# A hybrid attention and feed-forward block on one core: decays from empty rows, gate sums on quarters of the array, S1 in its own tile

## The chip, the cores and the metric

One Trainium2 chip, one core. The metric is the device time of one execution in microseconds, the median of several runs. The profile is of one execution, taken by the hardware profiler.

## The reference

One layer on x of 1024 frames by 1024 channels, all in float32. What matters here is the gated linear attention: 4 heads, 16 chunks of 64 frames each.

```
a = rmsnorm(x); proj = a @ w_in      # q, k, v, r, a_low (16), su, sv, g_gla, g_sgu
logit = a_low @ w_gate_up + b_gate
log_a = log_sigmoid(logit) / 16      # (16 chunks, 64 frames, 4 heads, 128)
cum = cumsum(log_a) in each chunk;  tot = cum[last frame]
k_dec = k * exp(tot - cum);  upd = k_dec^T v (each chunk);  decay = exp(tot)
state = decay * state + upd;  o = q @ state   (every frame reads its chunk's end state)
```

Behind it come a normalisation of o and silu(r), a spatial gating unit on su and sv, two branch projections that are gated and added, w_out, and a SwiGLU block (w_ffn_in, w_ffn_out); both halves add to x through a normalisation.

## The kernel before

Every large product is a pair of output blocks made with seven block products in place of eight (class `Pair`): the input is split in quadrants a11, a12, a21, a22, sums of quadrants such as S1 = a21 + a22 are formed, and products m1 to m7 are accumulated. Each operand of a product is a rounded part (fp32r, written by ScalarE, line 85) and the rest (written by VectorE, line 86), so that one product of 128 x 128 by 128 x 512 is three matmuls (lines 109 to 111: high by high, low by high, high by low; tiles ah and al for the mixer's input, hh and hl for the feed-forward's). The first two pairs run in the order 1, 2, 5, 7, 6, 4, 3, two pairs in turn. `Stream.run(n, fill)` issues n products and after each steps background generators: the decays, the rows of k, the scan and others put their matmuls between the products. The order on each engine is set by the framework's scheduler from the priorities that this order of issue gives and from when operands are expected; `tc.issue_after` holds something back behind a named instruction.

Of the input, `tile` (line 159) transposes four blocks of 128 columns into the raw quadrants, `first` splits a11 and a12 (operands of m1 and m2), `second` (line 177) splits a22 (operand 4), adds a21 to a22 in place (line 181) and splits the sum (operand 5), and `rest` (line 184) forms operands 7, 6 and 3 from the sum, by subtractions in place.

The low-rank gate input (16 columns of w_in): `low_rank_weights` loads them, forms differences and splits them into `wah`, 64 columns of weights; `low_rank_sums` (line 457) makes two halves with 16 matmuls each from the split operands 1, 2, 5 and 4. They are called behind the fourth and the sixth product. `low_rank` (line 460) loads `w_gate_up` and `b_gate` into `wg` with three transfers of GpSimd's queue, and copies the sums into `al`, 96 rows: high part, low part, ones. `decays` (line 479) goes head by head: eight matmuls of 96 rows give the logits (line 491, tile lg), ScalarE takes Abs, Exp and Ln, VectorE the minimum and difference (line 500), the result is split (lh, ll). Then 16 matmuls with `chunksr` of two columns sum each chunk (line 508, tile tot) and ScalarE exponentiates them into `decay`; 4 matmuls with the strictly lower matrix `laterr` give the sums over later frames (lines 517, 518, tile gg), whose exponentials go to HBM (kd_d, line 390) and come back in `k_rows` (tile kdl), where k is scaled.

`scan` (line 537) takes two blocks of 128 frames in a round p: `update` (line 559, tile u, two banks) on halves of the array's rows, four state steps on VectorE (line 577), four readouts (line 586, tile o, one bank) on halves of its columns, then transpositions (ot). Small products share a pool of four PSUM banks (`tbank`).

The feed-forward input goes the same way (tiles hraw, hh, hl, `Hs`), with `Hs.rest` behind six products.

Of the kernel before, what the change touches and what calls it, by code (L numbers as in the profile page):

```python
# [8 lines left out]
F32 = mybir.dt.float32  # L9
F32R = mybir.dt.float32r  # L10
# [21 lines left out]
def hybrid_block(ctx, tc, I, out):  # L32
# [20 lines left out]
    kd_d = dram("kd_d", [HEADS, P, S])  # L53
    u_d = dram("u_d", [KT, P, S])
# [87 lines left out]
    class Operands:  # L142
# [34 lines left out]
        def second(self, tt):  # L177
            cols = slice((tt % 4) * P, (tt % 4) * P + P)
            a21, a22 = (self.raw[1, c][:, :, cols] for c in range(2))
            self.put(4, a22, cols)  # L180
            nc.vector.tensor_tensor(out=a22, in0=a21, in1=a22, op=ALU.add)
            self.after = self.put(5, a22, cols)

        def rest(self):
            a11, a12, a21, s1 = self.raw[0, 0], self.raw[0, 1], self.raw[1, 0], self.raw[1, 1]
# [122 lines left out]
    class Stream:  # L308
# [58 lines left out]
    chunks = cst.tile([P, 2], F32, name="chunks")  # L367
    nc.vector.memset(chunks, 0.0)
    nc.vector.memset(chunks[0:64, 0:1], 1.0 / 16)
    nc.vector.memset(chunks[64:128, 1:2], 1.0 / 16)  # L370
    chunksr = cst.tile([P, 2], F32R, name="chunksr")
    nc.vector.tensor_copy(chunksr, chunks)
    decay = cst.tile([P, HEADS, NT * 2], F32, name="decay")
# [66 lines left out]
    def low_rank_weights():  # L440

        wa = pl.tile([P, 12, 16], F32, tag="L", name="wa")
        nc.gpsimd.dma_start(out=wa[:, 0:8], in_=w_in[:, OA : OA + 16].rearrange("(k p) c -> p k c", p=P))
        wah = pl.tile([P, 12, 64], F32R, tag="L", name="wah")
        nc.gpsimd.tensor_copy(wah, zero.broadcast_to([P, 12 * 64]).rearrange("p (k c) -> p k c", k=12))
        with tc.issue_after(A.after[1].ins):
            nc.vector.tensor_tensor(out=wa[:, 8:12], in0=wa[:, 4:8], in1=wa[:, 0:4], op=ALU.subtract)
            split(wah[:, :, 0:16], wah[:, :, 32:48], wa)
        low["w"] = wah

    def low_rank_sums(half, terms):

        low[half] = tbank(f"al_{half}")
        for n, (m, c) in enumerate(terms):
            for i in range(8):
                k, part = i // 2, A.hl[m][i % 2]
                nc.tensor.matmul(low[half][0:64], lhsT=low["w"][:, c * 4 + k, :], rhs=part[:, k],
                                 start=n == 0 and i == 0, stop=n == 1 and i == 7)

    def low_rank():  # L460
        with tc.issue_after(A.last.ins):
            al = slot("al", (96, S))
            nc.gpsimd.memset(al[64:96, :], 1.0)
            wg = slot("wg", (96, 512))
            nc.gpsimd.memset(wg, 0.0)
            nc.gpsimd.dma_start(out=wg[0:16, :], in_=I["w_gate_up"][0])
            nc.gpsimd.dma_start(out=wg[32:48, :], in_=I["w_gate_up"][0])
            nc.gpsimd.dma_start(out=wg[64:65, :], in_=I["b_gate"][0:1, :])
            vr = slot("vr", (24, P))
            nc.gpsimd.dma_start(out=vr[0:8], in_=I["sgu_ln_g"][0].rearrange("g (c p) -> (g c) p", p=P))  # L470
            nc.gpsimd.dma_start(out=vr[8:16], in_=I["sgu_ln_b"][0].rearrange("g (c p) -> (g c) p", p=P))
            nc.gpsimd.dma_start(out=vr[16:24], in_=I["gla_norm"][0].rearrange("g (c p) -> (g c) p", p=P))
        b = tbank("vecT")
        nc.tensor.transpose(b[:, 0:24], vr, ident[0:24, 0:24])
        nc.vector.tensor_copy(vecs, b[:, 0:24])
        for half in range(2):
            nc.scalar.activation(al[0:64, half * 512 : half * 512 + 512], low[half][0:64], AF.Copy)
        return al, wg

    def decays(al, wg):  # L480
        lh = slot("lh", (P, 1024), F32R)
        ll = slot("ll", (P, 1024), F32R)
        e = slot("e")
        for h in range(HEADS):
            lgs = []
            for q in range(2):
                lg = tbank(f"lg_{h}{q}")
                lgs.append(lg)
                for j in range(4):
                    tt = q * 4 + j  # L490
                    nc.tensor.matmul(lg[:, j * P : (j + 1) * P], lhsT=al[:, tt * P : (tt + 1) * P],
                                     rhs=wg[:, h * P : (h + 1) * P], start=True, stop=True)
                nc.scalar.activation(e[:, q * 512 : q * 512 + 512], lg, AF.Abs)
            yield
            yield
            nc.scalar.activation(e, e, AF.Exp, scale=-1.0)
            nc.scalar.activation(e, e, AF.Ln, bias=ones)
            for q in range(2):
                cols = slice(q * 512, q * 512 + 512)
                nc.vector.scalar_tensor_tensor(out=e[:, cols], in0=lgs[q], scalar=0.0, in1=e[:, cols], op0=ALU.min,  # L500
                                               op1=ALU.subtract)
# [602 lines left out]
```

## Time and profile before

| | |
|---|---|
| median of 3 runs | 1580.73 us (1579.82 to 1582.79) |
| profiled execution | 1581.19 us |
| its span, first to last instruction | 1579.3 us |
| mean granted TensorE clock | 0.991 of full |
| busy: TensorE, VectorE, ScalarE, GpSimd | 1545.6, 1134.2, 659.1, 168.2 us |
| instructions | 19738, of which 7103 matmuls |

The profile gives, for each engine, the time in which it worked; TensorE's matmuls overlap, so the duration of one (0.39 us for 512 columns) is longer than the distance to the next. The granted clock is the share of the full TensorE clock (2.4 GHz) that the chip allowed in a stretch; it has two levels here, full and half (1.2 GHz). An idle time in front of an instruction is shown with the instruction that ended it.

### The profile page before, as it was taken

The page shows a single profiled execution, that of the slowest core. Times are in us where ns is not written, and L with a number is a line of the kernel's source. Part 1 is how long each engine was busy: PE and PEld are TensorE (multiplying, and loading weights), DVE is VectorE, ACT ScalarE, POOL GpSimd, SP SyncE. Part 2 cuts the span into 40 slices and gives each one's busy share as a digit, 9 for nine tenths or more (in the row PEclk, how much of TensorE's full clock was granted, in tenths as well). Part 3 has the DMA queues.
Part 4 walks back from the last instruction along what each step waited for, and adds up shares of the span by engine and source line. Part 5 has one row for each costly group of instructions (what it writes and reads, how often), then busy time and mean ns, then how long its engine had stood idle before and what let it go on. Part 6 is the DMA issues. An engine that isn't in the chain of part 4 may idle for free.

```text
span 1579.3 us, 19738 instructions
## 1 busy us (share of the span) xinstructions
PE 1545.6 (98%) x7103; PEld 1261.5 (80%) x7103; DVE 1134.2 (72%) x1856; ACT 659.1 (42%) x1073; POOL 168.2 (11%) x251
## 2 busy tenths in 40 slices
PE   7999999999999999999999989999999999999997
PEld 5688777777788888888887877888888888888886
DVE  7855666767698788657697779787777776565547
ACT  8466433435444443444343654333333333354442
POOL 2100011112021112000000120111111100000001
PEclk9999999999999999999999998999999999999999
DMA  4232253636546455498982532565655543785653
GB/s 162 76 100 94 94 173 108 200 101 219 167 163 199 127 173 154 164 333 289 334 289 89 183 128 74 182 203 178 192 187 190 184 134 108 272 281 168 223 168 127
DMA packets 181236, 275.92 MB, mean 175 GB/s; under 512 B 10249, under 2 KB 108065, under 8 KB 181138
## 3 DMA queue, kind: packets, MB, share of 16 engines
q1 hardware_dynamic: 157714, 190.35, 38.1%
q0 software_dynamic: 23424, 84.30, 14.6%
q8 instruction: 56, 0.92, 0.2%
q14 instruction: 42, 0.34, 0.1%
HBM read 188.37 MB, written 86.25 MB: 174 GB/s over the span
## 4 chain that ended last, share of the span: by engine, by line
PE 91%; DVE 4%; ACT 2%; DMA 1%; issue 1%; POOL 0%; SPq 0%; DVEq 0%; POOLq 0%; ACTq 0%
PE f_m L110 9%; PE f_m L109 9%; PE f_m L111 9%; PE fo L109 4%; PE fo L111 4%; PE fo L110 4%; PE g_m L111 3%; PE g_m L109 3%; PE g_m L110 3%; PE kq_m L109 2%; PE v_m L110 2%; PE su_m L109 2%; PE v_m L109 2%; PE v_m L111 2%; PE sv_m L109 2%; PE kq_m L110 2%
## 5 line engine op out<-in xcount | busy, mean ns | idle before, releaser
L109 PE MATMUL f_m<-hh,w_f 128*128 128x512 f32 x616 | 241.2, 392 | 7.0 <-ACT hh L85 7.0
L110 PE MATMUL f_m<-hl,w_f 128*128 128x512 f32 x616 | 240.4, 391 | 0.0
L111 PE MATMUL f_m<-hh,w_f 128*128 128x512 f32 x616 | 238.2, 391 | 0.0
L109 PEld LDWEIGHTS f_m<-hh,w_f 128*128 128x128 f32 x616 | 116.3, 189 | 32.1 <-ACT hh L85 8.0
L110 PEld LDWEIGHTS f_m<-hl,w_f 128*128 128x128 f32 x616 | 116.4, 189 | 24.2
L111 PEld LDWEIGHTS f_m<-hh,w_f 128*128 128x128 f32 x616 | 116.2, 189 | 24.2
L111 PE MATMUL fo<-fow,foa 128*128 128x512 f32 x308 | 119.8, 389 | 0.0
L110 PE MATMUL fo<-fow,foa 128*128 128x512 f32 x308 | 119.8, 389 | 0.0
L109 PE MATMUL fo<-fow,foa 128*128 128x512 f32 x308 | 118.2, 389 | 0.0
L85 ACT ACTIVATE w_f<-wsum_f 128x512 fp32r<-128x512 f32 x88 | 55.4, 630 | 107.1 <-PE f_m L111 60.5
L109 PE MATMUL g_m<-ah,w_g 128*128 128x512 f32 x224 | 88.3, 394 | 0.0
L111 PE MATMUL g_m<-ah,w_g 128*128 128x512 f32 x224 | 87.8, 393 | 0.0
L110 PE MATMUL g_m<-al,w_g 128*128 128x512 f32 x224 | 87.7, 392 | 0.0
L85 ACT ACTIVATE w_f<-raw_f 128x512 fp32r<-128x512 f32 x66 | 41.4, 630 | 103.2 <-PE f_m L111 88.8
L86 DVE TENSOR_TENSOR foa<-fora,foa 128x1024 fp32r<-128x1024 f32 (+1 forms) x42 | 47.6, 1133 | 43.2 <-ACT foa L85 43.0
L85 ACT ACTIVATE foa<-fora 128x1024 fp32r<-128x1024 f32 (+1 forms) x42 | 41.5, 988 | 75.4 <-DMA fora<-fs_d 66.1
L274 DVE TENSOR_TENSOR f_o<-f_m,f_u 128x512 f32<-128x512 f32 x62 | 42.7, 689 | 40.2 <-PE f_m L111 40.0
L86 DVE TENSOR_TENSOR w_f<-wsum_f,w_f 128x512 fp32r<-128x512 f32 x88 | 60.4, 687 | 14.6 <-ACT w_f L85 14.1
L111 PEld LDWEIGHTS fo<-fow,foa 128*128 128x128 f32 x308 | 57.8, 188 | 12.1
L110 PEld LDWEIGHTS fo<-fow,foa 128*128 128x128 f32 x308 | 57.8, 188 | 12.1
L109 PEld LDWEIGHTS fo<-fow,foa 128*128 128x128 f32 x308 | 57.8, 188 | 11.8
L86 DVE TENSOR_TENSOR w_f<-raw_f,w_f 128x512 fp32r<-128x512 f32 x66 | 45.4, 688 | 21.0 <-ACT w_f L85 19.9
(384 smaller groups left out, 3743.0 us busy)
## 6 DMA issues: line engine op xcount, KB each, us to landing
raw_f<-in_w_ffn_in SPq DMA_DIRECT2D x88, 256.0 KB, 3.4
fora<-fs_d SPq DMA_DIRECT2D x35, 512.0 KB, 4.5
w2e<-in_w_ffn_out SPq DMA_DIRECT2D x44, 256.0 KB, 4.4
fs_d<-f_o POOLq DMA_DIRECT2D x22, 512.0 KB, 3.2
ws_d<-w2e POOLq DMA_DIRECT2D x22, 512.0 KB, 3.7
forw<-ws_d SPq DMA_DIRECT2D x20, 512.0 KB, 4.7
raw_g<-in_w_in SPq DMA_DIRECT2D x16, 512.0 KB, 4.6
g_d<-g_o POOLq DMA_DIRECT2D x16, 512.0 KB, 4.0
```

The source lines that it names most:

```text
L85: a = nc.scalar.activation(hi, src, AF.Copy)
L86: return a, nc.vector.tensor_tensor(out=lo, in0=src, in1=hi, op=ALU.subtract)
L109: nc.tensor.matmul(acc, lhsT=lh, rhs=rh, start=first, stop=False, skip_group_check=onto)
L110: nc.tensor.matmul(acc, lhsT=lh, rhs=rl, start=False, stop=False, skip_group_check=onto)
L111: nc.tensor.matmul(acc, lhsT=ll, rhs=rh, start=False, stop=last, skip_group_check=onto)
L274: tt(out=o, in0=in0, in1=in1, op=ALU.add)
```

## The change

1. S1 gets a tile of its own (quad(2, 0)); the split of a22 moves out of `second` into a new `fourth`, which is called behind the low-rank sums (and, for the feed-forward input, behind four products).
2. The low-rank sums are 32 plain f32 matmuls on raw quadrants with 32 columns of weights, each quarter of the array's columns taking 256 frames, issued behind the fourth product and before operand 4. The splits of the weights go. VectorE evacuates the bank once, adding 1 in the rows that carry the bias.
3. The logits are made for two heads at once, on quarters of the array's rows, in four banks; `wg` is loaded by eight transfers instead of three. A dependency by hand lets the first matmul of a pair of heads wait until all four banks are free.
4. The chunk totals (`tot`) go. The column of `later` that belongs to the last frame of each chunk, which was empty, is set to 1/16, so that row 63 (and 127) of gg holds the total, and its exponential the decay. Those rows are stored to `dec_d`, the other 63 rows of each chunk to kd_d, whose missing rows are filled with ones. Behind the fourth head `dt` is loaded from `dec_d` and one transposition (decT) brings the decays into place.
5. `update` of the next round is issued right behind the readouts of this one.

```diff
         def second(self, tt):
             cols = slice((tt % 4) * P, (tt % 4) * P + P)
-            a21, a22 = (self.raw[1, c][:, :, cols] for c in range(2))
-            self.put(4, a22, cols)
-            nc.vector.tensor_tensor(out=a22, in0=a21, in1=a22, op=ALU.add)
-            self.after = self.put(5, a22, cols)
+            s1 = self.quad(2, 0)[:, :, cols]
+            nc.vector.tensor_tensor(out=s1, in0=self.raw[1, 0][:, :, cols], in1=self.raw[1, 1][:, :, cols], op=ALU.add)
+            self.after = self.put(5, s1, cols)
+
+        def fourth(self, tt):
+            cols = slice((tt % 4) * P, (tt % 4) * P + P)
+            self.put(4, self.raw[1, 1][:, :, cols], cols)
...
+    for c in range(2):
+        nc.gpsimd.memset(later[c * 64 : c * 64 + 64, c * 64 + 63 : c * 64 + 64], 1.0 / 16)
...
+    def low_rank_sums():
+
+        low["al"] = tbank("al")
+        for k in range(KT):
+            for j in range(4):
+                a = A.raw[1 - j // 2, k // 4][:, k % 4, j % 2 * 256 : j % 2 * 256 + 256]
+                nc.tensor.matmul(low["al"][j * 32 : j * 32 + 32, 0:256], lhsT=low["w"][:, k], rhs=a, start=k == 0,
+                                 stop=k == KT - 1)
...
+            nc.vector.tensor_reduce(out=bias, in_=ident[:, 16:P:32], op=ALU.add, axis=mybir.AxisListType.X)
+            nc.vector.tensor_scalar(out=al, in0=low["al"][:, 0:256], scalar1=bias, scalar2=None, op0=ALU.add)
+        nc.gpsimd.memset(wg, 0.0)
+        for j in range(4):
+            nc.gpsimd.dma_start(out=wg[j * 32 : j * 32 + 16, :], in_=I["w_gate_up"][0])
+            nc.gpsimd.dma_start(out=wg[j * 32 + 16 : j * 32 + 17, :], in_=I["b_gate"][0:1, :])
...
+        for c in range(2):
+            nc.gpsimd.dma_start(out=kd_d[:, c * 64 + 63], in_=allone[0:HEADS])
...
+            for i in range(2):
+                for j in range(4):
+                    rows = slice(j * 32, j * 32 + 32)
+                    with tc.issue_after(first.ins) if first else ExitStack():
+                        mm = nc.tensor.matmul(lgs[j][:, i * 256 : i * 256 + 256], lhsT=al[rows, i * P : (i + 1) * P],
+                                              rhs=wg[rows, h * P : (h + 2) * P], start=True, stop=True)
...
-            tot = tbank(f"tot_{h}")
-            for tt in range(NT):
-                for part, first in ((lh, True), (ll, False)):
-                    nc.tensor.matmul(tot[:, 2 * tt : 2 * tt + 2], lhsT=part[:, tt * P : (tt + 1) * P], rhs=chunksr,
-                                     start=first, stop=not first)
-            nc.scalar.activation(decay[:, h], tot[:, 0 : NT * 2], AF.Exp)
...
-            store(kd_d[h], kd)
+            for c in range(2):
+                store(kd_d[h, c * 64 : c * 64 + 63], kd[c * 64 : c * 64 + 63])
+                store(dec_d[h, c : c + 1], kd[c * 64 + 63 : c * 64 + 64])
             yield
+            yield
+            yield
+        dt = slot("dt", (HEADS * 16, P))
+        nc.gpsimd.dma_start(out=dt, in_=dec_d.rearrange("h c (t k) -> (h c t) k", k=P))
+        for _ in range(4):
+            yield
+        b = tbank("decT")
+        nc.tensor.transpose(b[:, 0 : HEADS * 16], dt, ident[0 : HEADS * 16, 0 : HEADS * 16])
+        nc.vector.tensor_copy(decay.rearrange("p h c t -> p (h c t)"), b[:, 0 : HEADS * 16])
...
+        ubs = update(0)
+        yield
         for p in range(NT // 2):
             tt = 2 * p
-            ubs = update(tt)
-            yield
...
                 for i in (2, 1, 0):
                     read(i)
+                if tt + 2 < NT:
+                    ubs = update(tt + 2)
...
-    stream.run(4)
     low_rank_weights()
-    low_rank_sums(1, ((1, 0), (2, 1)))
+    stream.run(4)
+    low_rank_sums()
+    for tt in (0, 1, 2, 3):
+        A.fourth(tt)
     stream.run(2)
-    low_rank_sums(0, ((5, 0), (4, 2)))
     A.rest()
...
-    fstream.run(6)
+    fstream.run(4)
+    fstream.prepare(6)
+    for tt in (0, 1, 2, 3):
+        Hs.fourth(tt)
     Hs.rest()
```

The instructions on TensorE around the first change. Names: su0_m5 is the accumulator of product 5 of the first su pair, ah5 and al5 the two parts of operand 5, al_434 the bank of the low-rank sums. Before, behind the last product of m1 and m2:

```order
L110 MATMUL su1_m1_390<-al2_189,w_su12_270 128x512
L111 MATMUL su1_m1_390<-ah2_188,w_su12_270 128x512
L109 MATMUL su0_m5_472<-ah5_299,w_su05_407 128x512
L109 MATMUL su1_m5_492<-ah5_299,w_su15_426 128x512
L109 MATMUL su0_m7_554<-ah7_526,w_su07_469 128x512
L109 MATMUL su1_m7_571<-ah7_526,w_su17_489 128x512
L110 MATMUL su0_m5_472<-al5_300,w_su05_407 128x512
L111 MATMUL su0_m5_472<-ah5_299,w_su05_407 128x512
```

In the changed kernel the end of the low-rank sums stands at that place:

```order
L452 MATMUL al_434<-araw01_179,wa_363 32x256 x2
L452 MATMUL al_434<-araw11_289,wa_363 32x256 x2
L452 MATMUL al_434<-araw01_179,wa_363 32x256 x2
L110 MATMUL su0_m5_482<-ah5_293,w_su05_398 128x512
L110 MATMUL su1_m5_502<-ah5_293,w_su15_417 128x512
L110 MATMUL su0_m7_547<-ah7_519,w_su07_479 128x512
L110 MATMUL su1_m7_564<-ah7_519,w_su17_499 128x512
L111 MATMUL su0_m5_482<-al5_294,w_su05_398 128x512
```

The 32 low-rank matmuls stood 39 rows further on, all in one piece; they now stand between m2 and the first products of m5 and m7.

The second place on TensorE, before: the chunk totals of the first head among the kq products.

```order
L111 MATMUL kq0_m7_769<-ah4_294,w_kq04_809 128x512
L109 MATMUL kq0_m7_769<-ah4_294,w_kq04_809 128x512
L110 MATMUL kq0_m7_769<-al4_295,w_kq04_809 128x512
L508 MATMUL tot_0_845<-chunksr_125,ll_752 128x2
L508 MATMUL tot_0_845<-chunksr_125,lh_751 128x2
L508 MATMUL tot_0_845<-chunksr_125,ll_752 128x2
```

In the changed kernel there are none; the transposition of the decays stands among v products, ahead of the transpositions of k (kt):

```order
L112 MATMUL v1_m6_1308<-ah6_527,w_v16_1253 128x512
L110 MATMUL v1_m6_1308<-ah6_527,w_v16_1253 128x512
L111 MATMUL v1_m6_1308<-al6_528,w_v16_1253 128x512
L541 MATMUL decT_1291<-ident_106,dt_1250 128x64
L553 MATMUL kt_00_1297<-ident_106,kq0_o0_842 128x128 x4
L112 MATMUL v1_m6_1308<-ah6_527,w_v16_1253 128x512
L110 MATMUL v1_m6_1308<-ah6_527,w_v16_1253 128x512
```

Between the last gg matmul and decT the new order has 56 regular matmuls.

The third place, on TensorE in the scan of the first head, rounds 0 and 1, before. The last of four readouts and the next update:

```order
L586 MATMUL o_00_1474<-st_000_1450,kq0_o1_842 64x256
L111 MATMUL su2_m1_1516<-ah1_184,w_su21_1456 128x512
L109 MATMUL su2_m1_1516<-ah1_184,w_su21_1456 128x512
L110 MATMUL su2_m1_1516<-al1_185,w_su21_1456 128x512
L111 MATMUL su2_m1_1516<-ah1_184,w_su21_1456 128x512
L109 MATMUL su2_m1_1516<-ah1_184,w_su21_1456 128x512
L110 MATMUL su2_m1_1516<-al1_185,w_su21_1456 128x512
L111 MATMUL su2_m1_1516<-ah1_184,w_su21_1456 128x512
L559 MATMUL u_020_1531<-v_00_1382,kk_0_1349 128x256
L559 MATMUL u_021_1532<-v_00_1382,kk_0_1349 128x256
L559 MATMUL u_020_1531<-v_00_1382,kk_0_1349 128x256
L559 MATMUL u_021_1532<-v_00_1382,kk_0_1349 128x256
```

And in the changed kernel:

```order
L608 MATMUL o_00_1439<-st_003_1416,kq0_o1_860 64x256
L608 MATMUL o_00_1439<-st_002_1415,kq0_o1_860 64x256
L608 MATMUL o_00_1439<-st_001_1414,kq0_o1_860 64x256
L608 MATMUL o_00_1439<-st_000_1413,kq0_o1_860 64x256
L581 MATMUL u_020_1444<-v_00_1329,kk_0_1296 128x256
L581 MATMUL u_021_1445<-v_00_1329,kk_0_1296 128x256
L581 MATMUL u_020_1444<-v_00_1329,kk_0_1296 128x256
L581 MATMUL u_021_1445<-v_00_1329,kk_0_1296 128x256
```

The seven products between the readouts and the next update are gone; such neighbours were 5 before and are 12 now.

## Rows read from the trace of the kernel before

**Rows 1.** the page, busy time of each engine, and the chain's shares by engine
```profile
PE 1545.6 (98%) x7103; PEld 1261.5 (80%) x7103; DVE 1134.2 (72%) x1856; ACT 659.1 (42%) x1073; POOL 168.2 (11%) x251
...
PE 91%; DVE 4%; ACT 2%; DMA 1%; issue 1%; POOL 0%; SPq 0%; DVEq 0%; POOLq 0%; ACTq 0%
```

**Rows 2.** waits by engine: engine, line, what it waited for, us in total, times, longest
```profile
PE f_m L109 <- ACT hh L85: 7.0, 2, 4.9
```

**Rows 3.** timeline of PE: start us, us, engine, line, tiles, shapes, count, [idle before, releaser]
```profile
37.05 0.39 PE L111 MATMUL su_m<-ah,w_su 128*128 128x512 f32 x1
41.15 0.73 PE L109 MATMUL su_m<-ah,w_su 128*128 128x512 f32 x2 [3.71 <-ACT ah L85]
43.31 1.22 PE L109 MATMUL su_m<-ah,w_su 128*128 128x512 f32 x2 [1.43 <-ACT ah L85]
...
54.73 0.40 PE L457 MATMUL al<-ah,wah 128*64 128x512 f32 x1
...
62.09 0.39 PE L109 MATMUL su_m<-ah,w_su 128*128 128x512 f32 x1
...
80.47 0.39 PE L109 MATMUL kq_m<-ah,w_kq 128*128 128x512 f32 x1
```

**Rows 4.** windows: stretch, its us, busy of PE, PEld, DVE, ACT, POOL, granted clock, DMA
```profile
43.00:49.00 6.00, 5.66 (x13) 4.02 (x14) 6.00 (x8) 2.54 (x4) 0.00 (x0) 0.50 0.32 87
836.00:840.00 4.00, 1.45 (x6) 1.05 (x6) 4.00 (x8) 0.63 (x1) 0.00 (x0) 1.00 0.43 131
947.00:957.00 10.00, 6.89 (x15) 4.96 (x16) 8.82 (x9) 6.89 (x8) 0.00 (x0) 0.50 0.17 50
```

**Rows 5.** timeline of ACT, the first stage
```profile
40.47 0.63 ACT L85 ACTIVATE ah<-araw 128x512 fp32r<-128x512 f32 x1 [1.12 <-DVE araw L181]
```

**Rows 6.** timeline of DVE, the first stage
```profile
39.75 0.68 DVE L181 TENSOR_TENSOR araw<-araw,araw 128x512 f32<-128x512 f32 x1
...
40.95 2.35 DVE L194 TENSOR_TENSOR araw<-araw,araw 128x1024 f32<-128x1024 f32 x2
```

**Rows 7.** timeline of PE, logits and chunk totals of the first head
```profile
85.44 1.95 PE L491 MATMUL lg<-wg,al 96*128 96x128 f32 x16
...
99.00 0.25 PE L508 MATMUL tot<-chunksr,lh 128*128 128x2 f32 x1
...
100.45 0.25 PE L508 MATMUL tot<-chunksr,ll 128*128 128x2 f32 x1
```

**Rows 8.** timeline of PE, updates (u) and readouts (o) of the scan
```profile
197.46 1.13 PE L559 MATMUL u<-v,kk 64*128 64x256 f32 x4
...
248.70 0.39 PE L110 MATMUL v_m<-al,w_v 128*128 128x512 f32 x1
249.02 1.08 PE L586 MATMUL o<-st,kq_o 128*64 128x256 f32 x8
250.03 1.14 PE L559 MATMUL u<-v,kk 64*128 64x256 f32 x8
...
251.44 0.39 PE L109 MATMUL v_m<-ah,w_v 128*128 128x512 f32 x1
```

**Rows 9.** tile kd: the store to kd_d on GpSimd, duration min/median/max ns, landing us
```profile
L390 POOL DMA_DIRECT2D kd_d<-kd x4: 531/531/533, 104.4 to 161.4; - x4
...
DMA to landing us min/median/max: 2.9/2.9/4.9
```

**Rows 10.** timeline of PE, start of the feed-forward part
```profile
947.99 1.22 PE L109 MATMUL f_m<-hh,w_f 128*128 128x512 f32 x2 [4.92 <-ACT hh L85]
951.33 1.22 PE L109 MATMUL f_m<-hh,w_f 128*128 128x512 f32 x2 [2.12 <-ACT hh L85]
```

**Rows 11.** timeline of ACT, the same stretch
```profile
942.67 1.08 ACT L170 ACTIVATE hraw<-tp_h 128x512 f32<-128x512 f32 x2 [0.58 <-PE tp_h L169]
...
947.31 0.63 ACT L85 ACTIVATE hh<-hraw 128x512 fp32r<-128x512 f32 x1 [1.78 <-DVE hraw L181]
```

**Rows 12.** timeline of DVE, the same stretch
```profile
946.60 0.68 DVE L181 TENSOR_TENSOR hraw<-hraw,hraw 128x512 f32<-128x512 f32 x1
```

More of the change, by code (lines that the diff above doesn't have):

```diff
@@ L440, in low_rank_weights @@
     def low_rank_weights():
[L442 to L458, printed above, removed]
+        wa = pl.tile([P, KT, 32], F32, tag="L", name="wa")
+        nc.gpsimd.memset(wa, 0.0)
@@ L473, in low_rank @@
         b = tbank("vecT")
         nc.tensor.transpose(b[:, 0:24], vr, ident[0:24, 0:24])
-        nc.vector.tensor_copy(vecs, b[:, 0:24])
-        for half in range(2):
-            nc.scalar.activation(al[0:64, half * 512 : half * 512 + 512], low[half][0:64], AF.Copy)
+        low["free"] = nc.vector.tensor_copy(vecs, b[:, 0:24])
+        allone = slot("ones_rows", (8, S))
+        nc.gpsimd.memset(allone, 1.0)
+        for c in range(2):
+            nc.gpsimd.dma_start(out=kd_d[:, c * 64 + 63], in_=allone[0:HEADS])
@@ L482, in decays @@
         ll = slot("ll", (P, 1024), F32R)
-        e = slot("e")
-        for h in range(HEADS):
[L485 to L493, printed above, removed]
-            yield
[L495 to L501, printed above, removed]
+        es = [slot(f"e{i}") for i in range(2)]
@@ new lines, in decays, with logits @@
+        free = low["free"]
+        def logits(h):
+            lgs = [tbank(f"lg_{h}{j}") for j in range(4)]
+            first = None
+            for i in range(2):
[4 more added lines that the diff above has]
+                                              rhs=wg[rows, h * P : (h + 2) * P], start=True, stop=True)
+                    if not first:
+                        first = mm
+                        tc.add_manual_dep(first.ins, free.ins.name,
+                                          mybir.DependencyInfo(mybir.DependencyClass.Sync, mybir.DependencyReason.DATA),
+                                          reason="all banks free")
+            return [lg.rearrange("p (i h t) -> p h i t", i=2, h=2) for lg in lgs]
@@ new lines, in decays @@
+        for h in range(HEADS):
+            e = es[h % 2]
+            quarter = lambda x, j: x[:, j * 256 : j * 256 + 256].rearrange("p (i t) -> p i t", i=2)
+            if h % 2 == 0:
+                lgs = logits(h)
+                for i in range(2):
+                    for j in range(4):
+                        nc.scalar.activation(quarter(es[i], j), lgs[j][:, i], AF.Abs)
+                yield
+                yield
+                for i in range(2):
+                    nc.scalar.activation(es[i], es[i], AF.Exp, scale=-1.0)
+                    nc.scalar.activation(es[i], es[i], AF.Ln, bias=ones)
+                    for j in range(4):
+                        free = nc.vector.scalar_tensor_tensor(out=quarter(es[i], j), in0=lgs[j][:, i], scalar=0.0,
+                                                              in1=quarter(es[i], j), op0=ALU.min, op1=ALU.subtract)
```

45 lines of the change are left out of this document (19 added, 26 removed).

## The prediction, on record before the changed kernel ran

> **What bounds the kernel now.** I read the page's busy shares and its chain first. TensorE is busy 98% of the span and holds 91% of the chain that ended last; VectorE is at 72%, ScalarE at 42%, GpSimd at 11% [rows 1]. So a microsecond taken from TensorE's stream is a microsecond of the run, unless it only becomes a wait, and work on other engines counts only where TensorE stands idle. Then TensorE's waits: the largest is 7.0 us in two pieces, at the start of the feed-forward products, on ScalarE's rounded copies [rows 2]. The timeline shows the same pattern early on, 3.71 and 1.43 us, and gives the stream's pitch: from 62.09 to 80.47 the order has 81 regular products, 0.227 us each [rows 3]. Last the granted clock: it is full nearly everywhere, and half for some microseconds behind each of the two waits [rows 4].
>
> The sum is made against the profiled execution, 1581.2 us (span 1579.3); the median of the runs is 1580.73, so it stands 0.03% from it. About 0.2% (3 us) is what a measurement of this kernel tells from no change.
>
> **The change, part by part.**
>
> *Start (S1 in its own tile, low-rank sums ahead of the h5 products).* The last m2 product starts at 37.05, so the next could at 37.28; the low-rank sums start at 54.73 [rows 3]. The order has 39 products between (17.45 us; at 0.227 they need 8.85), so 8.6 us are lost: the two idles, and the half clock behind them [rows 4]. The first idle waits for S1's last quarter, added only at 39.75, and its rounding at 40.47 [rows 5, 6]: the sum overwrote a22, so it waited until a22's own split was done. In its own tile it waits for neither; VectorE and ScalarE have it some 2 us earlier, near 38.7. In the new order the low-rank sums, which need only raw copies, fill TensorE to about 41.2, h5 follows at once, and h7, wanted at 41.6, is ready near 41.3 (its first subtraction moves up from 40.95 by one addition and one split, 1.2 us, and waits for the low-rank sums of k = 0 to 3, read by 39.3). I take the whole 8.6 us; bounds 1 (idle moves to h7 and the clock still falls) and 8.6.
>
> *Low-rank sums.* Before, 32 products from 54.73 to 62.09, 7.36 us [rows 3]. After, 32 plain f32 products with 32 columns of weights and 256 of data. The nearest price of plain f32 is the logits: 16 passes of 128 columns in 1.95 us, the last 0.275 [rows 7], so 0.112 a pass, 0.223 for 256 columns, 0.447 for a product of two passes. One behind the other: 14.3 us; four quarters at once: 3.57. No row shows quarters; halves it shows. An update of 8 records (two halves abreast) lasts 1.14 us, the same as 4 records in one bank (1.13) [rows 8], so a second tile costs nothing. That being the nearest row, I take four abreast. Entering and leaving a tiled mode costs something: from 248.70 to 251.44, two neighbouring groups take 2.74 us; less two products (0.45) and 8 slots of 0.223 leave 0.5 for three changes, 0.17 each [rows 8]. So 3.57 + 0.34 = 3.9, a gain of 3.45; bounds 0 (two abreast, 7.15 + 0.34) and, serial, a loss of 7.3.
>
> *Logits.* Before, 64 passes x 0.112 = 7.2 us. After, 16 products of 0.447 on row quarters; the first pair of heads goes in two visits (three quarters, then the fourth, since it waits for its weight rows), the second in one: 3 x (0.89 + 0.34) = 3.7, a gain of 3.5; two abreast 6.4 us, a gain of 0.8.
>
> *Chunk totals.* 64 matmuls of two columns vanish. Fourteen of them start between 99.00 and 100.45 [rows 7], 0.112 apart: 7.1 us. The products for the decay matrix stay as they were, the totals come from rows that were empty. Their exponentials ride in the kd rows; what is added is off TensorE: 12 more stores and a load on GpSimd at 0.53 us each [rows 9], 7 us on an engine idle 89% of the time. The transposition that brings the decays back costs 0.11 + 0.34 = 0.45. It could wait: behind the last of its inputs come two exponentials (1.2), four issues (2.1), a landing of 2.9 [rows 9], one more issue and a small load (2.2): 8.4 to 9 us, against 56 products (12.7 us) that the order sets between. I cost the wait at nothing; if the landing takes its maximum, 4.9 [rows 9], it is still 2 us short of showing.
>
> *Updates beside readouts.* Five of 12 already lie beside one; after, all 12. Each new join saves one change of mode, 7 x 0.17 = 1.2; four updates stay cut in two. I take 1.0, bounds 0 and 1.5. Here the wait is moved, not added: an update issued early holds two of four banks longer.
>
> *Start of the feed-forward part.* The same tile change. TensorE waits 4.92 and 2.12 us [rows 10]; the last two raw copies end at 943.75 [rows 11], the sum that could follow starts only at 946.60 [rows 12], behind the split of what it overwrites, and h5's last quarter is rounded at 947.31 [rows 11]. Without that wait it is third on ScalarE behind the copies: 943.8 + 3 x 0.55 = 945.4 against 947.94. A gain of 2.5; h7 moves with it, so the second wait stays. The half clock of 947 to 957 [rows 4] I leave in place, since about 5 us of idle remain.
>
> Sum: 8.6 + 3.45 + 3.5 + 7.1 - 0.45 + 1.0 + 2.5 = 25.7; 1581.2 - 25.7 = **1555.5 us**.
>
> **Rivals.**
> (1) *Full clock in the feed-forward start.* Between 836 and 840 TensorE worked 1.45 of 4 us, idle otherwise, and the clock stayed full [rows 4]; now the first wait shrinks to about 2.4. Against: a second of the same size stands right behind it. It gives back some 3.5 us: the stretch from 947 to 957 holds 6.9 us of TensorE work at half speed [rows 4]. 1552.
>
> (2) *Quarters run two abreast.* Only halves are shown. It loses 3.6 on the low-rank sums and 2.7 on the logits: 1562. Fully serial it loses 10.7 and 8: 1574. The Trainium skill ("TensorE: Matmul & The Clock Gate", Part 3, packing small matmuls) states 3.07 times the speed for four row tiles of 32, not 4; by that, as an estimate, the two parts cost 1.9 us more and the sum comes to 1557.4. The halves in the trace do better than such a ratio, and no run shows quarters.
>
> (3) *The start still stalls.* h7's margin is 0.3 us and its buffers come free only when the low-rank sums have read them. Three us of idle and the half clock behind it (3.5): 1562; all of it, 1564.
>
> (4) *The decays come late.* If GpSimd's queue is held up by 9 us or more, TensorE idles some 5 us at the transposition and the clock falls: 1564.
>
> (5) *Slower: the early updates starve the banks.* They hold two of four banks from one readout to the next scan step, and transposes, readouts and later updates queue for the other two; TensorE's stream is in order, so all products behind stop too. It decides if each of the 12 places costs over 25.7 / 12 = 2.1 us; at 3 us each it is 1555.5 + 36 = 1591.5. For: only four banks. Against: in the five places that are like this already, the update follows its readout with no idle [rows 8].
>
> That the joins don't do what the words say (five were there already) changes 1 us at most, and is inside the forecast.
>
> **How the numbers follow.** Forecast 0.42; (1) 0.15; (2) 0.15; (3) 0.13; (4) 0.09; (5) 0.06. The range goes from 1551 (1, with the small bounds) to 1566 (the upper ends of 3 and 4); outside lie serial quarters, (5) and two misfortunes at once. Faster by over 0.2% are the forecast and (1) to (4), 0.94, less 0.01 for mishaps that come together; (5) gives 0.05 to slower and, with that, 0.02 to no change.
>
> **What would show it.** Right: no idle between 37 and 50 us and a full clock there; the low-rank group near 3.9 us; two logits pairs near 3.7 together; no matmul of two columns; first kq product near 68.4 instead of 80.47; one idle of 2.4 instead of 4.9 ahead of the feed-forward products. Wrong: starts of the four quarters not within some 10 ns of each other; a TensorE wait that names h7's rounding, the decays' load or a bank; a new half-clock stretch.

## The result, and the profile after

| | before | changed |
|---|---|---|
| median | 1580.32 us (1579.82 to 1582.79, 4 runs) | 1565.74 us (1564.08 to 1566.11, 4 runs) |
| profiled execution | 1581.19 us | 1564.08 us (span 1562.3, clock 0.992) |

The changed kernel takes 0.9903 of the time of the one before, 95% interval 0.9885 to 0.992: 14.6 us less by the medians, 17.1 us by the profiled executions. The forecast was 1555.5; the result lies 10 us above it and 0.3 us under the top of the range. The direction was right; the size was six tenths of what the sum had.

The page first, busy time and the shares of the chain, in answer to [rows 1]:

```profile
PE 1529.0 (98%) x7040; PEld 1245.7 (80%) x7040; DVE 1136.6 (73%) x1861; ACT 650.4 (42%) x1070; POOL 179.1 (11%) x273
...
PE 90%; DVE 5%; ACT 2%; DMA 1%; issue 1%; SPq 0%; POOL 0%; DVEq 0%; POOLq 0%; ACTq 0%
```

TensorE still bounds the run. VectorE's share of the chain went from 4 to 5%, the only share that grew, so the next view is TensorE's waits (engine, tile and line, what it waited for, us in total, times, longest):

```profile
PE f_m L110 <- ACT hh L86: 5.2, 2, 2.6
PE st L715 <- DVE bias L700: 2.5, 1, 2.5
...
PE sv_m L110 <- ACT sv_u L285: 1.3, 1, 1.3
```

The 7.0 us of [rows 2] are 5.2 now; the waits of st and sv_m are new. Smaller ones stand at the start, where 3.71 and 1.43 us were lost to ah before. TensorE's timeline shows it, in answer to [rows 3]:

```profile
36.75 0.39 PE L112 MATMUL su_m<-ah,w_su 128*128 128x512 f32 x1
37.07 3.66 PE L452 MATMUL al<-araw,wa 128*32 128x256 f32 x64
40.66 0.73 PE L110 MATMUL su_m<-ah,w_su 128*128 128x512 f32 x2
42.14 0.73 PE L110 MATMUL su_m<-ah,w_su 128*128 128x512 f32 x2 [0.74 <-ACT ah L86]
...
57.93 0.39 PE L112 MATMUL su_m<-ah,w_su 128*128 128x512 f32 x1
59.72 0.47 PE L110 MATMUL su_m<-ah,w_su 128*128 128x512 f32 x1 [1.40 <-ACT w_su L86]
...
61.42 0.50 PE L110 MATMUL su_m<-ah,w_su 128*128 128x512 f32 x1 [0.41 <-DVE su_u L291]
...
71.53 0.39 PE L110 MATMUL kq_m<-ah,w_kq 128*128 128x512 f32 x1
```

From the last m2 product to the first kq product TensorE took 80.47 - 37.05 = 43.42 us before and takes 71.53 - 36.75 = 34.78 now: 8.64 us less, where the start and the low-rank sums together were to give 12.05. The low-rank sums did their part: 64 records (32 products of two passes) in 3.66 us, and the four of a step, one on each quarter, start 6 to 7 ns apart. Of the 3.41 us that are missing, three idles are 2.55: 0.74, 1.40 and 0.41. The rest goes with them, since an idle is counted only from the end of the product before it: from 57.93 to 59.72 are 1.79 us, where two products one behind the other start 0.23 apart, so that the idle of 1.40 costs 1.56. ScalarE and VectorE say why, in answer to [rows 5, 6]; ScalarE:

```profile
33.91 1.28 ACT L308 ACT_TABLE_LOAD   x1
...
37.22 0.60 ACT L171 ACTIVATE araw<-tp_a 128x512 f32<-128x512 f32 x1
...
41.03 1.06 ACT L86 ACTIVATE ah<-araw 128x1024 fp32r<-128x1024 f32 x1 [1.02 <-DVE araw L198]
...
58.48 0.63 ACT L86 ACTIVATE w_su<-wsum_su 128x512 fp32r<-128x512 f32 x1 [4.57 <-DVE wsum_su L249]
59.02 1.14 ACT L86 ACTIVATE w_su<-raw_su 128x512 fp32r<-128x512 f32 x2
```

And VectorE, with two rows from further down that the text comes back to:

```profile
38.57 0.69 DVE L181 TENSOR_TENSOR araw<-araw,araw 128x512 f32<-128x512 f32 x1
...
39.78 1.22 DVE L198 TENSOR_TENSOR araw<-araw,araw 128x1024 f32<-128x1024 f32 x1
...
55.35 2.35 DVE L87 TENSOR_TENSOR al<-as,ah 128x1024 fp32r<-128x1024 f32 x2
57.69 0.68 DVE L249 TENSOR_TENSOR wsum_su<-raw_su,wsum_su 128x512 f32<-128x512 f32 x1
...
398.21 2.15 DVE L700 SCALAR_TENSOR_TENSOR bias<-rowsum,vecs,bsp 128x128 f32<-128x128 f32 x8
400.28 0.68 DVE L278 TENSOR_TENSOR sv_o<-sv_m,sv_u 128x512 f32<-128x512 f32 x1
```

The first idle is operand 7's. Its first subtraction (L198) starts at 39.78, 1.2 us sooner than before; it takes 1.22 us and the rounding behind it (41.03) 1.06, so the operand is there at 42.09, and TensorE stood ready at 41.4. S1's last addition also came 1.2 us sooner (39.75 to 38.57) and not 2: it no longer waits for a22's split, but the last raw copy (L171) now stands behind a table load on ScalarE, at 37.22, and VectorE has a weight sum (L246, 37.97) in between. That alone cost nothing, since S1's rounding was done at 40.00 and product 5 starts at 40.66.

The second idle: product 4's weight sum (L249) starts at 57.69, right behind two splits of operand 3 (2.35 us); its rounding on ScalarE follows at 58.48, and behind that, in ScalarE's order, the rounding of product 3's weights (59.02, the first of two done near 59.6), for which TensorE stands until 59.72. The third waits for an evacuation (su_u) on VectorE.

The logits and the decays, on TensorE, in answer to [rows 7]:

```profile
77.39 0.39 PE L110 MATMUL kq_m<-ah,w_kq 128*128 128x512 f32 x1
77.71 1.15 PE L495 MATMUL lg<-aw 32*128 32x256 f32 x12
...
79.12 0.39 PE L112 MATMUL kq_m<-ah,w_kq 128*128 128x512 f32 x1
...
107.89 1.15 PE L495 MATMUL lg<-aw 32*128 32x256 f32 x16
...
144.47 0.27 PE L541 MATMUL decT<-ident,dt 64*128 64x64 f32 x1
```

Twelve records on three quarters and sixteen on four take the same 1.15 us: the quarters run beside each other without loss. From 77.39 to 79.12 there are two regular products and the visit: 1.73 - 0.45 = 1.28 us a visit. The transposition of the decays has no idle in front of it.

Further on, still on TensorE, stands what the sum did not have:

```profile
382.07 0.50 PE L110 MATMUL sv_m<-ah,w_sv 128*128 128x512 f32 x1 [1.35 <-ACT sv_u L285]
...
396.68 1.02 PE L693 MATMUL rowsum<-wT,allone 128*128 128x512 f32 x2
397.54 0.49 PE L715 MATMUL st<-ident,sv_o 128*128 128x128 f32 x3
400.51 0.45 PE L715 MATMUL st<-ident,sv_o 128*128 128x128 f32 x1 [2.48 <-DVE bias L700]
```

The row sums of the spatial weights take one of the four shared PSUM banks. Three transpositions (st) go into the other three. The fourth needs the first bank again, and that is free when VectorE has made its eight bias operations (398.21, 2.15 us, in the rows above). That the three transpositions took one bank each is read from the order in which the pool hands out its banks; the profile shows the wait alone. The bank is not the whole of it either. The next product (sv_m) needs an evacuation (sv_o, 400.28, 0.68 us) that stands behind the same bias operations on VectorE, so by these rows TensorE would have stood until then with the bank free too; its weight load waits for that evacuation:

```profile
401.01 0.29 PEld L110 LDWEIGHTS sv_m<-ah,w_sv 128*128 128x128 f32 x1 [0.35 <-DVE sv_o L278]
```

Last the feed-forward start, and the granted clock of the stretches in question (us, busy of PE, PEld, DVE, ACT, POOL, clock, DMA), in answer to [rows 10, 4]:

```profile
931.61 0.73 PE L110 MATMUL f_m<-hh,w_f 128*128 128x512 f32 x2 [2.52 <-ACT hh L86]
...
934.97 1.22 PE L110 MATMUL f_m<-hh,w_f 128*128 128x512 f32 x2 [2.64 <-ACT hh L86]
```

```profile
50.00:62.00 12.00, 10.20 (x44) 7.65 (x43) 12.00 (x18) 4.59 (x7) 4.83 (x9) 1.00 0.02 5
62.00:66.00 4.00, 4.00 (x19) 3.33 (x18) 4.00 (x8) 1.48 (x3) 1.55 (x4) 1.00 0.78 244
400.00:408.00 8.00, 7.43 (x22) 5.70 (x23) 4.63 (x12) 2.10 (x4) 0.75 (x1) 0.57 0.19 66
822.00:830.00 8.00, 5.93 (x26) 4.89 (x27) 8.00 (x15) 0.91 (x2) 0.00 (x0) 1.00 0.41 131
932.00:941.00 9.00, 6.36 (x19) 4.74 (x18) 9.00 (x10) 5.96 (x8) 0.00 (x0) 0.62 0.20 58
```

From 50 to 62 VectorE worked 12.00 of 12 us. Behind the idle at 400 the clock is half for most of 8 us: 0.57 means half speed for 86% of them, some 6.4 of the 7.43 us of work, which costs about 3.2. The feed-forward start has half clock for some 6.8 us (0.62 of 9) instead of 10.

### The profile page after: what moved, and what is told of

Read it like the earlier page. It is cut to its first block, busy times and chain, and to the rows that moved or that the text cites. A ratio compares the mean times of both kernels' runs of the same rounds, so it can differ in the third digit from the quotient of the medians.

```text
span 1562.3 us, 19655 instructions
## 1 busy us (share of the span) xinstructions
PE 1529.0 (98%) x7040; PEld 1245.7 (80%) x7040; DVE 1136.6 (73%) x1861; ACT 650.4 (42%) x1070; POOL 179.1 (11%) x273
## 4 chain that ended last, share of the span: by engine, by line
PE 90%; DVE 5%; ACT 2%; DMA 1%; issue 1%; SPq 0%; POOL 0%; DVEq 0%; POOLq 0%; ACTq 0%
PE f_m L112 9%; PE f_m L110 9%; PE f_m L111 9%; PE fo L111 4%; PE fo L110 4%; PE fo L112 4%; PE g_m L110 3%; PE g_m L111 3%; PE g_m L112 3%; PE wo L112 2%; PE wo L110 2%; PE wo L111 2%; PE v_m L110 2%; PE kq_m L112 2%; PE kq_m L111 2%; PE v_m L112 2%
## 5 line engine op out<-in xcount | busy, mean ns | idle before, releaser
L86 ACT ACTIVATE w_f<-raw_f 128x512 fp32r<-128x512 f32 x66 | 41.4, 630 | 105.2 <-PE f_m L112 90.8
```

Source lines behind the costliest of these rows:

```text
L86: a = nc.scalar.activation(hi, src, AF.Copy)
```

## The experiments

The theory after this reading: the gain went into waits that the shorter background work brought about. A `yield` in the scan hands TensorE one more product; part 5 of the change drops one in each round but the first, so everything queued behind the scan comes a few products earlier, the row sums too. Each experiment ran beside the kernel before on the same chip; its medians there were 1581.01, 1581.52 and 1581.49 us for the three batches (e1 to e4, e5 to e8, e9 to e12). The second batch ran on another chip than the other two, so it is compared with e1 by the ratios.

### e1: the yield put back

```diff
         for p in range(NT // 2):
+            if p:
+                yield
```

> The changed kernel, with the one step of the background work that each round of the scan lost put back (updates still issued right behind the readouts). Theory 1 (the mixer's constants met the first gate transpositions because the background work ran some six products earlier; the fourth bank then waited for the row sums' bank): the idle of 2.48 us before a transposition st and the half clock behind it are gone, 1558 to 1560 us. Theory 2 (the early updates hold two of the four banks, and this starves the stage): the idle stays, 1564 to 1566 us.

Measured: 1560.35 us (1559.92 to 1561.41), ratio 0.9869 [0.9855, 0.9884]. Both late idles are gone; TensorE's timeline has the twelve transpositions for three banks in one piece, and the fourth bank's at 417.67 behind 24 products:

```profile
410.87 1.47 PE L717 MATMUL st<-ident,sv_o 128*128 128x128 f32 x12
```

The idles at 42 and 59 to 62 are as in the changed kernel, but here the clock fell behind the second:

```profile
62.00:66.00 4.00, 4.00 (x12) 3.10 (x11) 3.30 (x7) 0.00 (x0) 1.45 (x4) 0.59 0.78 242
```

What follows: one yield in each round gives back 5.4 of the ten missing microseconds, and the two late stalls go with it. No run tells the idle at sv_m from the one at st; both went together here and in e5. In the profiled executions the stalls and the half clock behind them were 1.35 + 2.48 + 3.2 = 7.0 us and the gain is 3.7: six updates are cut in two here instead of four, which takes back some 2.5 (e12 has the price of a cut), and the half clock at 62 some 1.6, so 2.9 would be left by these prices.

### e2: the updates issued late again

```diff
-        ubs = update(0)
-        yield
         for p in range(NT // 2):
+            ubs = update(tt)
+            yield
...
-                if tt + 2 < NT:
-                    ubs = update(tt + 2)
```

> The changed kernel with the updates issued at the start of their own round, as before. Theory 1: the idle before st is gone as well, but the seven joins are lost, 1 us: 1559 to 1561 us, some 1 us above the run with the step put back. Theory 2: clearly faster than the run with the step put back, which still holds the banks: 1558 to 1560 against 1564 to 1566.

Measured: 1566.66 us (1565.65 to 1568.02), ratio 0.991 [0.9893, 0.9927], 6 us above what the theory of e1 gave. The stall at st is gone, but six updates are cut in two, and other idles have come (1.35, 0.72, 0.53 and 0.51). That the early updates cost time fell; that the yields alone account for everything fell with it.

### e3: operand 3 behind product 4's weights, on top of e1

```diff
-    A.rest()
+    A.rest((7, 6))
+    stream.prepare(12)
+    with tc.issue_after(stream.order[1].fourth.ins):
+        A.rest((3,))
```

> As the run with the step put back, and the operand of product 3 (subtractions and splits) is held until the weights' sum for the second pair's product 4 has been issued. Theory 3 (VectorE is the bound between 50 and 62 us once the low-rank sums fill the first stall; the weights of product 4 wait behind operand 3's splits): the two idles of 1.40 and 0.41 us near 58 to 62 us vanish and the first kq product starts 2 us earlier, near 69.5; the run is 2 us faster than the one with the step put back. Rival (VectorE has too much work there, whatever its order): the idle comes back at product 3, the time is the same.

Measured: 1560.44 us (1559.16 to 1561.53), ratio 0.9869 [0.9854, 0.9883]: the time of e1. The idles of 1.40 and 0.41 went, and a split of the input on VectorE (al) was late in their place: 1.78 us of idle at 60.65, and 1.30 at 395 on the normalised readouts. With VectorE full from 50 to 62 (11.97 of 12 us here), the order only picks who waits.

### e4: S1's own tile alone, on the kernel before

```diff
-            self.put(4, a22, cols)
-            nc.vector.tensor_tensor(out=a22, in0=a21, in1=a22, op=ALU.add)
-            self.after = self.put(5, a22, cols)
+            s1 = self.quad(2, 0)[:, :, cols]
+            nc.vector.tensor_tensor(out=s1, in0=self.raw[1, 0][:, :, cols], in1=self.raw[1, 1][:, :, cols], op=ALU.add)
+            self.after = self.put(5, s1, cols)
+
+        def fourth(self, tt):
+            cols = slice((tt % 4) * P, (tt % 4) * P + P)
+            self.put(4, self.raw[1, 1][:, :, cols], cols)
```

> The kernel before with S1's own tile and the later split of a22 alone; low-rank sums where they were, totals, logits and updates as before. If the tile alone shortens the two starts: the first idle there falls from 3.71 to about 1.5 us, the wait for h7 stays, the clock falls or not: 2 to 8 us at the start, 2.4 us at the feed-forward start (idle of 4.92 becomes about 2.5): 1571 to 1577. Rival (only the low-rank sums in the gap help at the start): 1577 to 1578.

Measured: 1575.97 us (1575.14 to 1577.08, 6 runs), ratio 0.9968 [0.9956, 0.9979]; 5.0 us less than before. TensorE's two idles at the start are smaller, not gone (3.71 and 1.43 in [rows 3]):

```profile
38.64 0.73 PE L109 MATMUL su_m<-ah,w_su 128*128 128x512 f32 x2 [1.31 <-ACT ah L85]
...
40.59 1.15 PE L109 MATMUL su_m<-ah,w_su 128*128 128x512 f32 x2 [1.22 <-ACT ah L85]
```

So the tile by itself takes 2.6 of the 5.1 us of these two idles, and the clock still falls there (half from 41 to 44.5); the first kq product starts at 76.53, 3.9 us sooner than before. The feed-forward start has the idles of the changed kernel already (2.52 and 2.64). What else the changed kernel gains at the first start comes from the low-rank sums that stand in the gap.

### e5: the spatial constants twelve products earlier, instead of the yield

```diff
-    stream.run(42, 2)
+    stream.run(30, 2)
```

> The changed kernel as it is, with the mixer's constants queued 12 products earlier in the background work, so that the row sums stand far ahead of the gate transpositions st; nothing else differs. Theory 1 (only the meeting of row sums and transpositions in the four banks costs): the idle of 2.48 us before st and the half clock behind it go, the idle of 1.35 us at 381 may stay: 1559 to 1562 us. Rival (the background work runs too early as such, and the wait comes back elsewhere): 1564 to 1566 us.

Measured: 1564.93 us (1561.78 to 1567.15, 5 runs), ratio 0.989 [0.9877, 0.9903]. The idles at st and sv_m are gone, and a new one of 1.95 us stands at the transposed readouts, with half clock behind it:

```profile
394.49 1.08 PE L635 MATMUL ot<-ident,on 128*128 128x128 f32 x4 [1.95 <-DVE on L626]
```

```profile
394.00:400.00 6.00, 5.51 (x18) 4.09 (x19) 2.02 (x4) 4.29 (x7) 0.74 (x1) 0.72 0.94 317
```

The narrow form of the theory (one bank, met at one moment) would have given e1's time. The wider reading fits better: the change took slack out of a stretch in which several things become ready just in time. This run doesn't show which of them.

### e6: some weight sums on GpSimd, on top of e1

```diff
-            tt = nc.vector.tensor_tensor
+            tt = (nc.gpsimd if self.name in ("su0", "su1") and m in (7, 6, 4) else nc.vector).tensor_tensor
```

> As the run with the step put back, and six of the weights' sums of the first two pairs (0.68 us each on VectorE) are made on GpSimd. Theory 3 (VectorE has more work between 37 and 62 us than the products leave time for): 4.1 us leave VectorE, the idles near 58 to 62 us (1.8 us) and the half clock that sometimes follows go, the first kq product starts near 69 to 70 us, 2 to 3.5 us faster than the run with the step put back: 1557 to 1558.5. Rival (a sum on GpSimd takes so long, or slows VectorE so much, that product 7 or 6 waits): the same or slower, 1560 to 1564.

Measured: 1564.27 us (1562.55 to 1567.62), ratio 0.9893 [0.988, 0.9906]; 3.8 us above e1, nothing gained. A sum of 128 x 512 takes 0.68 us on VectorE, and on GpSimd:

```profile
31.44 1.68 POOL L241 TENSOR_TENSOR wsum_su<-raw_su,raw_su 128x512 f32<-128x512 f32 x1 [2.07 <-DVE w_su L87]
```

while VectorE, beside it, has

```profile
31.88 1.79 DVE L87 TENSOR_TENSOR w_su<-wsum_su,w_su 128x512 fp32r<-128x512 f32 x1
```

instead of 0.68 to 0.69. The VectorE operation begins 0.44 us after GpSimd's and ends 0.55 after GpSimd's end (33.12): it stood still until GpSimd was nearly done. The VectorE operations that begin beside the next two sums do the same (1.78 us each, at 34.19 and 38.30). The Trainium skill ("SBUF — State Buffer", "Who interferes with whom") has this as a rule: the two engines share a pair of ports, locked for a whole instruction, and a VectorE operation with two inputs in SBUF contends there. These rows agree with it. Work is not taken off VectorE this way.

### e7: operand 7 first at the feed-forward start, on top of e1

```diff
+    Hs.rest((7,))
     for tt in (0, 1, 2, 3):
         Hs.fourth(tt)
-    Hs.rest()
+    Hs.rest((6, 3))
```

> As the run with the step put back; in the feed-forward start the operand of product 7 is formed before operand 4 is split. Theory 4 (the second wait there, 2.64 us, is operand 7's, which stands on VectorE and ScalarE behind splits that are needed later): it shrinks by 0.6 to 1.8 us, since one ScalarE rounding and one or two VectorE splits leave the path; the half clock may go with it (3 us): 1 to 4 us faster than the run with the step put back. Rival (the table load and the two copies of f_o on ScalarE hold it): under 0.7 us.

Measured: 1564.03 us (1562.6 to 1565.25), ratio 0.9889 [0.9876, 0.9901]; 3.2 us above e1. TensorE's idles are 3.12 and 2.60 us, followed by 0.42 and 1.00. ScalarE shows what holds operand 7:

```profile
929.88 1.28 ACT L1017 ACT_TABLE_LOAD   x1
931.17 1.08 ACT L1017 ACTIVATE f_o<-f_m 128x512 f32<-128x512 f32 x2
932.14 4.08 ACT L86 ACTIVATE hh<-hraw 128x1024 fp32r<-128x1024 f32 x6
```

A table load and two evacuations (2.26 us) stand ahead of its rounding, on an engine that the changed kernel has busy 42% of the span. Order on VectorE was not what held it: its first subtraction starts at 929.23 there and takes 1.2 us.

### e8: both starts reordered, with GpSimd, on top of e1

The edits of e6 and e7, and for the first input also `A.rest((7,))` ahead of the fourth operand.

> The run with the step put back, with the sums on GpSimd and operand 7 ahead of operand 4 at both starts. If the gains add: the idles of 0.74 near 41 and 1.8 near 58 to 62 and a part of the 2.64 in the feed-forward start go: 1553 to 1557 us. Rival: operand 4 comes late and the idle returns at product 4 or 6: 1558 to 1562.

Measured: 1573.35 us (1567.59 to 1574.46, 6 runs), ratio 0.9941 [0.9927, 0.9955]: 11 us behind e1. One idle of 5.00 us ahead of 67.32 waits for an evacuation on VectorE, and the clock falls in it (0.74 over 62 to 75). The parts do not add.

### e9 and e10: the changed kernel and e1 once more, on one chip

Both without an edit of their own. The changed kernel:

> The changed kernel once more, beside the run with the step put back. Theory 5 (the waits are fixed by the order of the instructions, whether the clock falls behind them is not): the idles of 0.74, 1.40, 0.41, 1.35 and 2.48 us stand in the same places within 0.15 us, while the half-clock stretches behind those near 58, 398 and 822 us may come or not: 1563 to 1567 us. Rival (the waits are chance): other idles than those, or none.

Measured: 1566.53 us (1566.25 to 1567.29), ratio 0.9906 [0.9892, 0.9919], with the same idles (0.73, 1.43, 0.40, 1.35, 2.48). The clock is full at 62 to 66, as in the first profile, half for a shorter part of 400 to 408 than in the first profile (0.79 for 0.57), and half for part of 822 to 830, where the first profile had it full:

```profile
400.00:408.00 8.00, 6.28 (x23) 4.81 (x24) 5.59 (x15) 2.19 (x4) 0.75 (x1) 0.79 0.19 66
822.00:830.00 8.00, 5.44 (x18) 4.02 (x17) 8.00 (x15) 1.51 (x3) 0.00 (x0) 0.79 0.34 104
```

The kernel of e1:

> The run with the step put back, once more and beside the changed kernel. Theory 1: 4 to 6 us faster than the changed kernel, 1559.5 to 1561.5 us, with no idle between 62 and 800 us. Rival (the difference was the chip's): within 2 us of the changed kernel.

Measured: 1560.7 us (1559.91 to 1562.05), ratio 0.9869 [0.9855, 0.9882]; 5.8 us less than e9 on the same chip. What the yield is worth is settled: 5.4 us in the first pair of runs, 5.8 in the second.

### e11: e3, with kq's first weight sums held back

```diff
+                with tc.issue_after(A.last.ins) if self.name == "kq0" else ExitStack():
+                    tt(out=src, in0=(w12, w22)[m == 7], in1=(w11, w12)[m == 7], op=ALU.subtract)
```

> As the run in which operand 3 was held, and the first two weights' sums of kq are held until operand 3 is done. Theory 3: the idle of 1.78 us at product 3 shrinks to about 1.2, since one VectorE instruction of 0.6 us leaves the path, and nothing else moves: the same time within 1 us as the run with the step put back, the start 0.6 us earlier. Rival: the sums of kq come late and a product of kq waits.

Measured: 1560.68 us (1558.88 to 1562.14), ratio 0.9868 [0.9853, 0.9883]. The stall at 58 to 62 is gone without a successor there, but operand 7's idle is 0.96 and one of 1.03 has come at 92.8 (gg, on the split of the decays). No gain over e10.

### e12: the early updates alone, on the kernel before

Part 5 of the change, with the yield of each round kept as in e1.

> The kernel before with the updates issued right behind the readouts alone, no step of the background work lost; totals, logits, low-rank sums and S1 as before. The order has 12 joins instead of 5, and 2 updates cut in two visits where before had 4 and one more that takes its banks in turn. Theory 6 (a join saves a change of mode, 0.2 us; an update cut in two visits costs a whole further visit, 1.27 us, since one bank at a time takes as long as two): 1.4 + 2.5 to 3.8, so 4 to 5 us, 1576 to 1577. Rival (the forecast's term): 1 us, 1580; or new waits eat it, 1581 and more.

Measured: 1577.44 us (1576.06 to 1578.36, 8 runs), ratio 0.9972 [0.9962, 0.9982]; 4.05 us less than before. TensorE's timeline shows a joined update and a cut one:

```profile
201.50 1.08 PE L588 MATMUL o<-st,kq_o 128*64 128x256 f32 x8
202.51 1.13 PE L559 MATMUL u<-v,kk 64*128 64x256 f32 x8
...
323.08 1.13 PE L559 MATMUL u<-v,kk 64*128 64x256 f32 x4
324.58 1.13 PE L559 MATMUL u<-v,kk 64*128 64x256 f32 x4
```

Eight records take 1.13 us and four take 1.13: an update whose second bank is not free in time pays a whole visit more. From 323.08 to 324.58 one product (0.23) and one visit pass: 1.27. Here two updates are cut instead of four. Seven joins at 0.17, two visits at 1.27 and an idle of 0.5 us ahead of an r product, which only the kernel before has, make 4.2, near the 4.05.

## Why the prediction was right in direction and 10 us short in size

| term | forecast | measured in the profiles |
|---|---|---|
| start | 8.6 | 5.0 (8.64 less 3.7) |
| low-rank sums | 3.45 | 3.7 (7.36 less 3.68: 36.75 to 40.66 less one product) |
| logits | 3.5 | 3.4 (7.2 less 3 x 1.28) |
| chunk totals | 7.1 | 7.1 (gone) |
| transposition of the decays | -0.45 | no wait, 0.4 assumed |
| updates | 1.0 | 1.8 (what is left of the stretch below) |
| feed-forward start | 2.5 | 2.4 |
| new stalls near 380 to 408 | none | -7.0 |
| sum | 25.7 | 16.0 |

The stretch is that from the first kq product to the first ys product: 595.44 us before, 590.58 now, 4.86 less; with the stalls taken out 11.9 were gained there, of which logits, totals and transposition leave 1.8 for the updates: a remainder, not a measurement, and 0.5 of it an idle in front of an r product that went. The -7.0 are the first profile's; a run that removes the stalls and what else the yield moves gives back 5.4 to 5.8. The feed-forward start follows from the lead over the kernel before, 14.59 us at its first product and 16.97 at the first fo product. The profiled executions differ by 17.1; of the 1.1 that the table leaves, 0.3 were gained ahead of the start and 0.8 between ys and the feed-forward part, and I can't assign them.

- **Low-rank sums, logits: right, and rival (2) fell.** 64 slots of 0.223 would be 14.3 us one behind the other; they took 3.66, 3.9 times as fast. The halves of [rows 8] were the right row to go by. The rule of the Trainium skill beside rival (2) ("TensorE: Matmul & The Clock Gate", Part 3), 3.07 times for four row tiles, would by an estimate have made a visit of the logits 1.5 us (16 x 0.223 / 3.07 and the 0.34 of the mode); it took 1.28. Yet sixteen records in 1.15 us are 3.1 times as fast as sixteen slots of 0.223, and twelve records on three quarters took the same 1.15: the ratio fits a short group, of whose 1.28 us some 0.4 are its beginning and end, and not the long one.
- **Chunk totals and decays: right; rival (4) did not come.** The 64 matmuls went, and the transposition found its input there.
- **Start: the size was wrong.** The step that failed is "h5 follows at once, and h7, wanted at 41.6, is ready near 41.3". h5 did follow. h7's first subtraction moved up by 1.2 us, as the step says (40.95 to 39.78), but that does not make it ready near 41.3: before, its product started at 43.31 [rows 3], and 1.2 less is 42.1, where it now starts (42.14). The forecast's own rows had this; 41.3 is what is left if the 2 us expected of S1 are taken off, and S1 came 1.2 us sooner. So this wait, 0.74 us, is an error of the sum. Then a stall that no step looked for: the products of this stretch come up to 9 us sooner (kq at 71.53 for 80.47) and want their weights as much sooner, and VectorE, which makes them, has no time left there. Rival (3) had the place; its price, 6.5 us and more, was nearly twice the 3.6 that came, since the clock stayed full in this profile.
- **Feed-forward start: the first wait was right**, 2.52 us of idle for 2.4 forecast. That the whole term came out (2.4 for 2.5) is luck in part: the second wait grew from 2.12 to 2.64 us and one ahead of the last transpositions (tp_h) from 0.59 to 1.17, while the half clock, which the term had left in place, shrank from 10 to some 6.8 us. Rival (1), a full clock there, fell.
- **Updates: right in sum, incomplete in its parts.** The term priced the joins at 0.17 and left the cuts alone; by e12's rows a cut costs 1.27, the larger price. In the changed kernel as many updates are cut as before, four.
- **What the sum left out: 7.0 us.** Its unspoken step was that the stream behind the changed places keeps its order. In [rows 8] I looked at whether an update follows its readout, and not at what a yield less per round does to the generators queued behind the scan. e1 and e10 give back 5.4 to 5.8 us of it. Rival (5) had the mechanism, a bank that isn't free, at the wrong operation: not the updates starved, but a transposition that met the row sums.
- **The range held by 0.3 us, and that is luck in part.** Its upper end was made from rivals (3) and (4); (4) did not come, (3) came at about half its price, and the rest of the room was used up by the stalls near 400 us, which no rival names.

e1 also shows that the forecast was not to be had by mending that alone: 1560.4 to 1560.7 remains 5 us over it, of which some 3.6 are the start. Four tries at the start (e3, e6, e8, e11) did not get these. Of the versions tried e1 is the best, 5.4 to 5.8 us ahead of the changed kernel, 1.3% ahead of the one before; e3 and e11 equal it with more edits.

## What to carry to other kernels

When a stretch of the bounding engine gets shorter, ask two things of each place behind it: which engine makes its inputs, and whether that engine had time left in that stretch. Where two engines are full and their order is fixed, part of a further saving turns into waits (here some ten of 25.7 us); a step that seems idle, a yield that only lets one more product pass, may be the slack that keeps two users of a bank apart. Price small tiled products by the visit to the mode, since four records take as long there as eight.

## What the runs showed of the hardware beyond this

- The same idle does or does not lower the clock, from one execution of the same program to the next. Behind the idles of 1.40 and 0.41 us near 60 the clock stayed full in the changed kernel both times and fell in e1, and stayed full in e10. Further down, with one idle of 2.13 us ahead of 820.46 in e1 and one of 2.03 ahead of 818.96 in e10, it is the other way round; the same kernel, first e1, then e10:

```profile
818.00:826.00 8.00, 5.87 (x26) 4.61 (x25) 8.00 (x15) 1.42 (x3) 0.00 (x0) 1.00 0.44 132
818.00:826.00 8.00, 7.04 (x24) 5.66 (x25) 8.00 (x14) 0.69 (x2) 0.00 (x0) 0.79 0.34 108
```

The drops shown cost from 1.6 us (e1, 62 to 66) to 3.2 (the changed kernel, 400 to 408). The four times of one kernel lie 1.5 to 3 us apart in most runs here; that the drops make this spread isn't shown, since only one execution of each run was profiled.
- Four quarters of the array work beside each other as well for rows as for columns: 64 records in 3.66 us, 16 in 1.15.
- An elementwise sum on GpSimd holds up the VectorE operation that begins beside it until it is nearly done: 0.68 us became 1.79.
